# Strassen's seven products in the input projection of a conv and gMLP layer, with 1024-token blocks

## The chip, the cores and the metric

The kernel runs on one core of a Trainium2 chip. A time is that of one execution on the device in microseconds (us); the time shown for a kernel is the median of several. Engines: PE (TensorE, matrix products into PSUM), DVE (VectorE), ACT (ScalarE), POOL (GpSimd), and SP, whose queue issues nearly all DMAs. Each engine works through its own instructions in the order in which the program has them.

## The reference

```python
mod = c @ w_ada + b_ada
shift, scale, gate = jnp.split(mod, 3, axis=-1)
h = rmsnorm(x, g_pre) * (1.0 + scale) + shift          # 2048 tokens x 1024 channels
p = h @ w_in                                           # 8 projections of 1024 columns each
a = val * sigmoid(glu)                                 # val, glu, z, u, v, z2, gA, gB: columns of p
y = causal_depthwise_conv(a, conv_w) + conv_b          # 31 taps
y_a = (silu(layernorm(y)) * silu(z)) @ w_conv_out
v = layernorm(gelu(v))
s = einsum(tril(w_s), v) + b_s                         # per head, in chunks of 128 positions
y_b = (gelu(u) * s * silu(z2)) @ w_sgu_out
x = x + gate * ((sigmoid(gA) * y_a + sigmoid(gB) * y_b) @ w_o)
out = rmsnorm(x, g_final)
```

All is float32. PE gets the precision by parts: every operand is split into a high part (its copy in PE's 12-bit format, made by ACT) and a low part (what is left, a subtraction), and a product is three matmuls, high*high, high*low and low*high.

## The kernel before

The 2048 tokens go in four blocks of 512. In a block the kernel computes seven of the eight projections channel by channel (`unit`, L228: 128 columns against 512 tokens, 8 row tiles by 3 matmuls of 128x512, L232 to L234), and v token by token (`rows_unit`, L240, L244 to L246). The order in a block is: gate and value of the GLU, v, the other GLU pairs mixed with u and z2 (`step_uz`, which also does the position mixing, L588), then gB with w_b, z, gA with w_a, and w_o. That makes 56 + 16 units of the input projection and 24 units' worth of output products, 2112 matmuls of 128x512 a block and 8448 in all.

Weights come in pieces of 128x1024, loaded on SP's queue and split by ACT (L66) and DVE (L67), five pieces ahead at most (`take`, L213). The convolution is background work on DVE: 30 instructions of 128x512 for each of 8 channel tiles and each block (L487), read from a and accumulated in y, both in SBUF; two channel tiles take turns. They are spread between what DVE does for PE by `run_bg`, which lowers their priority. POOL does little: it copies 30 columns between blocks (L502, L505), and in the first 76 us it splits weights (L67) and scales x (L337).

In the first block the shift and scale of the conditioning come step by step: the products of c with w_ada are summed by DVE (L282, L286) and then over the partitions by PE (L296, L297), and each step's result feeds 21 matmuls of the first projections (L370, L371, L377). The LayerNorm sums over channels are pairs of matmuls with ones (`sums_of`, L107).

Of the kernel before, what the change touches and what calls it, by code (L numbers as in the profile page):

```python
# [7 lines left out]
F32 = mybir.dt.float32  # L8
# [4 lines left out]
PSUM = bass.MemoryType.PSUM  # L13

# [3 lines left out]
KT = D // P  # L18
T = 512
NB = SEQ // T  # L20
# [3 lines left out]
GC = 256  # L24
# [4 lines left out]
G_GLU, G_VAL = 0, 1  # L29
G_ZA, G_U, G_ZB, G_GA, G_GB = (8 + 4 * i for i in range(5))  # L30

# Columns of the packed per-channel parameters.
# [6 lines left out]
START = 7  # units whose sums the first block carries side by side, one bank each  # L39
LATER = 800  # by how much the background work yields to what is emitted after it  # L40
AHEAD = 5  # split weight pieces on chip
# [3 lines left out]
def hybrid_layer(  # L45
# [5 lines left out]
    ps = ctx.enter_context(tc.tile_pool(name="ps", bufs=8, space=PSUM))  # L51
# [3 lines left out]
    sm = ctx.enter_context(tc.tile_pool(name="sm", bufs=2))  # L55

    def bank():
        return ps.tile([P, 512], F32, tag="ps", name="bank")
# [3 lines left out]

    def split(dst, val, eng=nc.vector):
# [3 lines left out]
        eng.tensor_tensor(out=lo, in0=val, in1=hi.bitcast(F32), op=ALU.subtract)  # L67

# [9 lines left out]
    ones = const.tile([P, P], F32R, name="ones")  # L78
    nc.vector.tensor_copy(out=ones, in_=one.broadcast_to([P, P]))
# [3 lines left out]
    nc.gpsimd.memset(halo, 0.0)  # L83
    shift = const.tile([P, KT], F32, name="shift")
    gsc = const.tile([P, KT], F32, name="gsc")

    def rstd_of(ss, src):
        """ss <- 1 / sqrt(src / D + EPS)"""
        nc.scalar.activation(ss, src, AF.Sqrt, bias=eps_t, scale=1.0 / D)
        nc.vector.reciprocal(out=ss, in_=ss)  # L90

    def sums(val):
        """The sum of val over the partitions, on each of them: native float32."""
        pt = bank()
        nc.tensor.matmul(pt, ones.bitcast(F32), val, start=True, stop=True)  # L95
        return pt

    def parts(val):
        hi, lo = t512("hi", F32R), t512("lo", F32R)
        split((hi, lo), val)  # L100
        return hi, lo

    def sums_of(parts):
        """The same from the two parts; the ones are exact in one."""
        pt = bank()
        for i, part in enumerate(parts):
            nc.tensor.matmul(pt, ones, part, start=i == 0, stop=i == 1)  # L107
        return pt

# [1 line left out]
    def load_x(b):  # L111
        xn = big.tile([P, KT, T], F32, tag="yx", name="xn", bufs=1)
        for k in range(0, KT, 2):
            nc.sync.dma_start(
                out=xn[:, k : k + 2, :],
                in_=xt[k * P : (k + 2) * P, b * T : (b + 1) * T].rearrange(
                    "(k p) t -> p k t", p=P
                ),
            )
        return xn  # L120

    def squares_x(xn):
        rx = tmp.tile([P, T], F32, tag="rs", name="rx", bufs=1)
        for k in range(KT):
            if k == 0:
                nc.scalar.activation(rx, xn[:, k], AF.Square)
            else:
                q = t512("q")
                nc.scalar.activation(q, xn[:, k], AF.Square)
                nc.vector.tensor_tensor(out=rx, in0=rx, in1=q, op=ALU.add)  # L130
        return rx

    def make_ht(xn, rx, k):
        h = xn[:, k]
        nc.vector.tensor_tensor(out=h, in0=h, in1=rx, op=ALU.mult)
        nc.scalar.activation(
            h, h, AF.Identity, bias=shift[:, k : k + 1], scale=gsc[:, k : k + 1]
        )
        ht = big.tile([P, 2, T], F32R, tag="ht", name="ht", bufs=KT)
        split(ht, h)  # L140
        return ht

# [1 line left out]
    def pair(mat, g):  # L144
        return [mat[g, 0], mat[g, 1]]

    def rowsof(mat):
        return [mat[k * P : (k + 1) * P, :] for k in range(KT)]

    order = []  # L150
    for b in range(NB):
        if b == 0:
            order += [k for k in range(KT)]
            order += pair(w_in, G_VAL + 2)
        else:
            for g in range(4):
                order += pair(w_in, g)
        order += rowsof(w_v)
        for i, j in ((2, 0), (3, 1), (None, 2), (None, 3)):
            if i is not None:  # L160
                order += pair(w_in, G_GLU + 2 * i) + pair(w_in, G_VAL + 2 * i)
            order += pair(w_in, G_U + j) + pair(w_in, G_ZB + j)
        for i in range(4):
            order += pair(w_in, G_GB + i) + pair(w_b, i)
        for i in range(4):
            order += pair(w_in, G_ZA + i)
        for i in range(4):
            order += pair(w_in, G_GA + i) + pair(w_a, i)
        order += rowsof(w_o)
    ready = {}  # L170
    loaded = []
    state = {"prep": 0, "use": 0}

    def prep_load():
        n = state["prep"]
        state["prep"] += 1
        src = order[n]
        raw = wp.tile([P, 4 * GC], F32, tag="raw", name="raw", bufs=3)
        if isinstance(src, int):
            ks = slice(src % 4 * GC, (src % 4 + 1) * GC)  # L180
            half = src // 4
            nc.sync.dma_start(
                out=raw[:, : 3 * GC].rearrange("p (g c) -> p g c", c=GC),
                in_=w_in[0:3, half, :, ks].rearrange("g p c -> p g c"),
            )
            nc.sync.dma_start(
                out=raw[:, 3 * GC : START * P],
                in_=w_in[3, half, :, ks][:, : START * P - 3 * GC],
            )
        else:  # L190
            nc.sync.dma_start(out=raw, in_=src)
        loaded.append((n, raw))

    def prep_split():
        n, raw = loaded.pop(0)
        if n >= len(order) - (KT - AHEAD):
            # The last block's w_o stays whole; the input's tiles are free by then.
            ready[n] = []
            for h in range(2):
                w = big.tile([P, 2, T], F32R, tag="ht", name="wht", bufs=KT)  # L200
                split(w, raw[:, h * 512 : (h + 1) * 512])
                ready[n].append(w)
            return
        w = wp.tile([P, 2, 4 * GC], F32R, tag="whl", name="whl", bufs=AHEAD)
        ready[n] = w
        if n < KT:
            split(w[:, :, : START * P], raw[:, : START * P], nc.gpsimd)
        else:
            split(w, raw)

    def take(count):
        """The next pieces; whatever fits beside them is made too."""
        n = state["use"]  # L213
        state["use"] += count
        while loaded:
            prep_split()
        while state["prep"] < min(n + max(AHEAD, count), len(order)):
            prep_load()
            prep_split()
        return [ready.pop(n + i) for i in range(count)]  # L220

    def group():
        """The split weights of the next group: part, k tile -> [P, GC]."""
        hv = [w.rearrange("p s (k c) -> p s k c", c=GC) for w in take(2)]
        return lambda s, kt: hv[kt // 4][:, s, kt % 4, :]

    def unit(pt, w, sub, rhs):
        """pt[channel, token] = 128 columns of the group against rhs."""  # L228
        cs = slice(sub * P, (sub + 1) * P)
        for kt in range(KT):  # L230
            wh, wl = w(0, kt)[:, cs], w(1, kt)[:, cs]
            nc.tensor.matmul(pt, wh, rhs[kt][:, 0], start=kt == 0, stop=False)  # L232
            nc.tensor.matmul(pt, wh, rhs[kt][:, 1], start=False, stop=False)  # L233
            nc.tensor.matmul(pt, wl, rhs[kt][:, 0], start=False, stop=kt == KT - 1)  # L234

    def columns(w):
        """A piece of 1024 columns in halves."""
        return w if isinstance(w, list) else [w[:, :, n * 512 : (n + 1) * 512] for n in range(2)]
# [9 lines left out]
    def rows_units(pts, w, lhs, kt):  # L248
        w = columns(w)
        for (c, n), pt in pts.items():  # L250
            rows_unit(pt, w[n], lhs, kt, c)
# [570 lines left out]
```

## Time and profile before

| what | value |
|---|---|
| time, median of 3 runs | 2008.87 us (2008.4 to 2011.4) |
| span of the profiled execution, first to last instruction | 2006.4 us |
| PE busy | 98% |
| DVE busy | 79% |
| ACT busy | 41% |
| POOL busy | 6% |
| DMA, mean | 113 GB/s |

The profile is of one execution; the median of the runs is 2.5 us above its span, which is what lies around the first and the last instruction. A busy PE alone does not say that the kernel is bound by it: the rows of the windows and of the chain of waits have to show that no other engine's wait stands in between.

### The profile page before, as it was taken

The numbers are of one execution on the slowest core, as the hardware profiler recorded it, in microseconds if no ns is written. First come the engines' busy times: TensorE is split into PE (matmuls) and PEld (weight loads), VectorE is DVE, ScalarE is ACT, GpSimd is POOL, SyncE is SP. The second block draws the span as 40 slices with busy tenths as digits, with TensorE's granted clock in tenths as the row PEclk, the third lists the DMA queues.
The fourth block names the chain that finished last, engine by engine and source line by source line (L and its number), as shares of the span: only waits on it lengthen the run. The fifth ranks groups of instructions, "written<-read, shape, count | busy, mean of one in ns | idle before, by whom it ended". The sixth has DMA issues, their size and how long they took to land.

```text
span 2006.4 us, 22659 instructions
## 1 busy us (share of the span) xinstructions
PE 1970.9 (98%) x8784; PEld 1632.2 (81%) x8784; DVE 1581.3 (79%) x2158; ACT 813.0 (41%) x1021; POOL 129.5 (6%) x77
## 2 busy tenths in 40 slices
PE   5899999999999999999999999999999999999998
PEld 4688888888888888888888888888888888888886
DVE  7999999576499999367469999837638999964644
ACT  3433432465324343266332444236524343423632
POOL 3300000000001420000000012000000000000000
PEclk9999999999999999999999999999999999999999
DMA  7542222334242222224432222224343323232332
GB/s 277 196 139 95 84 95 95 105 135 138 99 143 95 84 95 95 97 72 162 143 137 95 95 95 93 86 94 136 106 139 134 100 90 98 91 98 92 103 112 79
DMA packets 67995, 226.55 MB, mean 113 GB/s; under 512 B 7088, under 2 KB 11312, under 8 KB 67888
## 3 DMA queue, kind: packets, MB, share of 16 engines
q1 hardware_dynamic: 67744, 224.95, 33.3%
q8 instruction: 68, 1.11, 0.2%
q14 instruction: 39, 0.32, 0.1%
q10 hardware_dynamic: 144, 0.16, 0.0%
HBM read 216.69 MB, written 8.39 MB: 112 GB/s over the span
## 4 chain that ended last, share of the span: by engine, by line
PE 95%; DMA 1%; DVE 1%; ACT 0%; issue 0%; ACTq 0%
PE bank L234 25%; PE bank L232 25%; PE bank L233 25%; PE bank L245 6%; PE bank L246 6%; PE bank L244 6%; PE bank L588 1%; DMA raw<-in_w_o 1%; PE bank L107 0%; DVE acc L286 0%; PE bank L95 0%; PE bank L377 0%; PE bank L371 0%; PE bank L370 0%; ACT wht L66 0%; DVE whl L67 0%
## 5 line engine op out<-in xcount | busy, mean ns | idle before, releaser
L232 PE MATMUL bank<-ht,whl 128*128 128x512 f32 x1736 | 678.7, 391 | 0.0
L234 PE MATMUL bank<-ht,whl 128*128 128x512 f32 x1736 | 675.5, 389 | 0.0
L233 PE MATMUL bank<-ht,whl 128*128 128x512 f32 x1736 | 675.5, 389 | 0.0
L487 DVE SCALAR_TENSOR_TENSOR y<-a,vec,y 128x512 f32<-128x512 f32 x960 | 658.1, 742 | 0.1
L67 DVE TENSOR_TENSOR whl<-raw,whl 128x1024 fp32r<-128x1024 f32 x343 | 418.3, 1221 | 268.3 <-ACT whl L66 267.9
L66 ACT ACTIVATE whl<-raw 128x1024 fp32r<-128x1024 f32 (+1 forms) x351 | 370.4, 1057 | 592.9 <-PE bank L234 326.2
L234 PEld LDWEIGHTS bank<-ht,whl 128*128 128x128 f32 x1736 | 325.9, 188 | 67.8
L233 PEld LDWEIGHTS bank<-ht,whl 128*128 128x128 f32 x1736 | 326.1, 188 | 66.8 <-issue 0.2
L232 PEld LDWEIGHTS bank<-ht,whl 128*128 128x128 f32 x1736 | 326.1, 188 | 66.7 <-issue 0.2
L502 POOL COPY a<-halo 128x30 f32<-128x30 f32 x32 | 61.8, 1951 | 900.1 <-DVE y L487 848.8
L246 PE MATMUL bank<-whl,ht 128*128 128x512 f32 x256 | 99.6, 389 | 0.0
L244 PE MATMUL bank<-whl,ht 128*128 128x512 f32 x256 | 99.6, 389 | 0.0
L232 PE MATMUL bank<-yb,whl 128*128 128x512 f32 x256 | 99.6, 389 | 0.0
L234 PE MATMUL bank<-yb,whl 128*128 128x512 f32 x256 | 99.6, 389 | 0.0
L233 PE MATMUL bank<-ya,whl 128*128 128x512 f32 x256 | 99.6, 389 | 0.0
L245 PE MATMUL bank<-whl,ht 128*128 128x512 f32 x256 | 99.6, 389 | 0.0
L233 PE MATMUL bank<-yb,whl 128*128 128x512 f32 x256 | 99.6, 389 | 0.0
L232 PE MATMUL bank<-ya,whl 128*128 128x512 f32 x256 | 99.6, 389 | 0.0
L234 PE MATMUL bank<-ya,whl 128*128 128x512 f32 x256 | 99.6, 389 | 0.0
L245 PE MATMUL bank<-whl,mg 128*128 128x512 f32 x232 | 90.3, 389 | 0.0
L244 PE MATMUL bank<-whl,mg 128*128 128x512 f32 x232 | 90.3, 389 | 0.0
L246 PE MATMUL bank<-whl,mg 128*128 128x512 f32 x232 | 90.2, 389 | 0.0
(144 smaller groups left out, 1928.6 us busy)
## 6 DMA issues: line engine op xcount, KB each, us to landing
raw<-in_w_in SPq DMA_DIRECT2D x218, 512.0 KB, 3.3
raw<-in_w_v SPq DMA_DIRECT2D x32, 512.0 KB, 3.4
raw<-in_w_b SPq DMA_DIRECT2D x32, 512.0 KB, 3.2
raw<-in_w_a SPq DMA_DIRECT2D x32, 512.0 KB, 3.5
raw<-in_w_o SPq DMA_DIRECT2D x32, 512.0 KB, 3.3
xn<-in_xt SPq DMA_DIRECT2D x16, 512.0 KB, 6.5
wa<-in_wada SPq DMA_DIRECT2D x16, 512.0 KB, 7.8
xo<-in_x SPq DMA_DIRECT2D x16, 512.0 KB, 5.6
```

What stands on the lines that cost most here:

```text
L66: nc.scalar.activation(hi, val, AF.Copy)
L67: eng.tensor_tensor(out=lo, in0=val, in1=hi.bitcast(F32), op=ALU.subtract)
L232: nc.tensor.matmul(pt, wh, rhs[kt][:, 0], start=kt == 0, stop=False)
L233: nc.tensor.matmul(pt, wh, rhs[kt][:, 1], start=False, stop=False)
L234: nc.tensor.matmul(pt, wl, rhs[kt][:, 0], start=False, stop=kt == KT - 1)
L244: nc.tensor.matmul(pt, xh, w[:, 0], start=kt == 0, stop=False)
L245: nc.tensor.matmul(pt, xh, w[:, 1], start=False, stop=False)
L246: nc.tensor.matmul(pt, xl, w[:, 0], start=False, stop=kt == KT - 1)
L487: nc.vector.scalar_tensor_tensor(out=yj, in0=a[:, k : k + T], scalar=col(V_CW, j * TAPS + k), in1=yj, op0=ALU.mult, op1=ALU.add,)
L502: nc.gpsimd.tensor_copy(out=a[:, :HALO], in_=halo[:, j, :])
L588: nc.tensor.matmul(pq[:, c * P : (c + 1) * P], vn[c][:, j * P : (j + 1) * P], wsT[:, j, :], start=True, stop=True,)
```

## The change

The whole function is written anew. What it does:

- **Blocks and the projection.** There are two blocks of 1024 tokens (s). Each of 28 `quad`s computes two column tiles (128 columns each) for both token halves by seven products of quarters instead of eight: each product is 4 row tiles by 3 matmuls, 84 matmuls in place of 96. Three operands of the products are sums of quarters of h (S1 to S4, made once a block on DVE), and the weights' sums (t1 to t4) are made for each quad from four raw pieces of 128x512. The results are added up in two PSUM banks; ACT copies three partial results a quad to SBUF (`snap`), DVE adds three times.
- **POOL** makes three of the four sums of weights and the low parts of six of the seven pieces of a quad; DVE makes those of t4.
- **Convolution.** 30 instructions of 128x1024 a channel tile, one chain at a time, accumulated in a PSUM tile of two banks (`cv`), with the first tap by ACT.
- **v first.** v is computed first, from two passes over each 512-token half; its split weights are written to memory in the first pass and read back whole (512 KB a piece of 12 matmuls), w_o likewise. The mixing results, the four gates' values and y_b go through memory and are loaded again.
- **adaLN.** Shift and scale are sums along rows on DVE (one instruction for 128x1024), with c on every partition; PE takes no part. The RMS and LayerNorm factors are made as columns: products with one (`col_sums`), root and reciprocal of 128x4, and `spread`, a diagonal matrix on DVE and a native float32 matmul.

```diff
+    def quad_piece(q, kind):
...
+            pool = nc.gpsimd
+            eng = nc.vector if kind == "t4" else pool
...
+            elif kind == "t1":
+                val = add(r(0, 0), r(0, 1), eng)
...
+            w = piece_tile()
+            split(w, val, eng)
...
+            a = bank()
+            prod(a, [take()], A11)
+            p1 = snap(a)
+            run_bg(2)
+            b = bank()
+            prod(b, [take()], A12)
+            tt(out=p1, in0=b, in1=p1, op=ALU.add)
+            c11(p1)
+            run_bg(2)
+            if pending:
+                pending.pop()()
+                run_bg(1)
+            c = bank()
+            prod(c, [take()], S1)
+            p5 = snap(c)
+            run_bg(2)
+            prod(a, [take()], S2, start=False)
+            p16 = snap(a)
...
+            prod(c, [take()], S4, start=False)
+            tt(out=p16, in0=c, in1=p16, op=ALU.subtract)
+            c12(p16)
...
+            prod(a, [take()], S3, start=False)
+            tt(out=p5, in0=p5, in1=a, op=ALU.subtract)
...
+            def end():
+                prod(a, [take()], A22, start=False)
+                c21(a)
...
+            def tap(k):
+                dst = a[:, :S] if k == HALO else cv[0]
+                nc.vector.scalar_tensor_tensor(
+                    out=dst, in0=a[:, k : k + S], scalar=col(V_CW, j * TAPS + k), in1=cv[0],
+                    op0=ALU.mult, op1=ALU.add,
+                )
...
+        v_half(pts, vn1, st1, 1)
+        mv1 = v_aggr(st1)
+        came = v_norm(vn1, mv1)[:, 0:1]
+        mixing(1, vn1, wsT, sbias)
...
+        for j in range(KT):
+            glu(j)
+            uz(j)
+            spilled(AF.Sigmoid, d_sa[j], d_sbg[j])
+        for i in range(KH):
+            spilled(AF.Silu, d_sz[2 * i], d_sz[2 * i + 1])
...
+        def ln_rstd(h):
+            hh = slice(h * T, (h + 1) * T)
+            pc = bank()
+            col_sums(rsq[0][:, hh], pc, 0, NC)
+            pr = spread(rstd_cols(pc[:, :NC], NC))
```

Three places of the programs' order, where a row is a line of the kernel, an operation, and the tile that it writes and those that it reads. The first is DVE in the middle of the projections. Before, two channel tiles of the convolution take turns (a is the input with its halo, y the sum, vec the taps' weights):

```order
L487 SCALAR_TENSOR_TENSOR y_3841<-a_4119,vec_73,y_3841 128x512 [waits DVE_49]
L67 TENSOR_TENSOR whl_4361<-raw_4359,whl_4361 128x1024 [waits DMAHW1_49,Activation_49]
L487 SCALAR_TENSOR_TENSOR y_3841<-a_4083,vec_73,y_3841 128x512 [waits DVE_49]
L487 SCALAR_TENSOR_TENSOR y_3841<-a_4119,vec_73,y_3841 128x512 [waits DVE_49]
L487 SCALAR_TENSOR_TENSOR y_3841<-a_4083,vec_73,y_3841 128x512 [waits DVE_49]
```

Now one chain in cv stands between the sums of the quads (L634, L648, L652), the gates (L732, L733) and t4's pieces (L88, L223):

```order
L676 SCALAR_TENSOR_TENSOR a_1741<-a_1741,vec_75,cv_1945 128x1024 [waits DVE_49]
L687 TENSOR_TENSOR s1_2327<-a_1310,a_1741 128x1024 [waits DVE_49]
L715 TENSOR_TENSOR a_2202<-snap_2284,sg_2403 128x512 [waits Activation_49]
L676 SCALAR_TENSOR_TENSOR cv_2408<-a_2202,vec_75,cv_2408 128x1024 [waits DVE_49,Activation_49]
L88 TENSOR_TENSOR whl_2454<-raw_2267,whl_2454 128x512 [waits PE_49,Activation_49]
L676 SCALAR_TENSOR_TENSOR cv_2408<-a_2202,vec_75,cv_2408 128x1024 [waits DVE_49]
L648 TENSOR_TENSOR snap_2449<-bank_2410,snap_2449 128x512 [waits PE_49]
L676 SCALAR_TENSOR_TENSOR cv_2408<-a_2202,vec_75,cv_2408 128x1024 [waits DVE_49] x2
L732 TENSOR_TENSOR snap_2367<-snap_2367,snap_2449 128x512 [waits Activation_49]
L652 TENSOR_TENSOR snap_2428<-snap_2428,bank_2348 128x512 [waits DMAHW1_49,PE_49]
```

The convolution of one channel tile ends just ahead of the row (L715) that gives the input of the next, so it fills the three quads between two GLU quads. The second place is POOL. Before it has, in the middle of the kernel, only copies of the halo:

```order
L502 COPY a_4575<-halo_81 128x30 [waits DVE_49,Activation_49,Pool_49]
L502 COPY a_4611<-halo_81 128x30 [waits DVE_49,Activation_49,Pool_49]
L505 COPY halo_81<-a_4575 128x30 [waits DVE_49,Pool_49]
L505 COPY halo_81<-a_4611 128x30 [waits DVE_49,Pool_49]
L502 COPY a_4916<-halo_81 128x30 [waits DVE_49,Activation_49]
```

Now it has nine instructions of 128x512 for a quad, here those of one quad (raw are its four raw pieces, whl split pieces):

```order
L88 TENSOR_TENSOR whl_1808<-raw_1806,whl_1808 128x512 [waits DVE_49,DMAHW5_49,PE_49,Activation_49]
L223 TENSOR_TENSOR raw_1806<-raw_1806,raw_1866 128x512 [waits DMAHW0_49,Pool_49]
L223 TENSOR_TENSOR raw_1866<-raw_1866,raw_1886 128x512 [waits DMAHW5_49,Pool_49]
L88 TENSOR_TENSOR whl_1829<-raw_1827,whl_1829 128x512 [waits DMAHW6_49,PE_49,Activation_49]
L88 TENSOR_TENSOR whl_1869<-raw_1806,whl_1869 128x512 [waits Activation_49]
L223 TENSOR_TENSOR raw_1806<-raw_1806,raw_1886 128x512 [waits Pool_49]
L88 TENSOR_TENSOR whl_1889<-raw_1806,whl_1889 128x512 [waits Activation_49]
L88 TENSOR_TENSOR whl_1907<-raw_1886,whl_1907 128x512 [waits PE_49,Activation_49]
L88 TENSOR_TENSOR whl_1925<-raw_1866,whl_1925 128x512 [waits Activation_49]
```

The halo copies have left POOL. The third place is PE behind v. Before, the next GLU products follow v's last matmuls, and the mixing comes four units later:

```order
L244 MATMUL bank_4137<-whl_4253,ht_3795 128x512
L245 MATMUL bank_4137<-whl_4253,ht_3795 128x512
L246 MATMUL bank_4137<-whl_4253,ht_3795 128x512
L232 MATMUL bank_4472<-ht_3557,whl_4289 128x512 [waits Activation_49]
L233 MATMUL bank_4472<-ht_3557,whl_4289 128x512
```

Now the mixing (L432) of the second token half stands right behind its v products (L312 to L314), and the quads come after it:

```order
L312 MATMUL bank_1023<-whl_1066,h_791 128x512
L313 MATMUL bank_1023<-whl_1066,h_791 128x512
L314 MATMUL bank_1023<-whl_1066,h_791 128x512
L432 MATMUL bank_1198<-wsT_730,vn_807 128x128 [waits DVE_49,PE_49]
L432 MATMUL bank_1206<-wsT_730,vn_807 128x128 [waits PE_49]
L432 MATMUL bank_1198<-wsT_730,vn_808 128x128 [waits DVE_49]
```

Nothing is left on PE between v's last product and the first instruction that reads v's normalized values. In the same way each `col_sums` (L146) of the convolution's LayerNorm is followed directly by its `spread` (L161).

## Rows read from the trace of the kernel before

**Rows 1.** The page: busy time, share of the span and instructions of each engine.

```profile
PE 1970.9 (98%) x8784; PEld 1632.2 (81%) x8784; DVE 1581.3 (79%) x2158; ACT 813.0 (41%) x1021; POOL 129.5 (6%) x77
```

**Rows 2.** Windows: busy us (instructions) of PE, PEld, DVE, ACT, POOL; clock, DMA.

```profile
0.00:100.00 100.00, 71.98 (x290) 57.08 (x291) 86.75 (x128) 35.48 (x44) 33.23 (x29) 0.95 0.68 236
20.00:24.00 4.00, 3.61 (x10) 2.91 (x11) 3.63 (x5) 1.18 (x2) 2.74 (x2) 1.00 1.06 386
661.93:1149.35 487.42, 487.42 (x2185) 404.81 (x2184) 381.13 (x513) 202.24 (x252) 47.59 (x16) 1.00 0.32 108
1999.00:2006.40 7.40, 0.01 (x1) 0.00 (x0) 2.63 (x5) 1.74 (x4) 0.00 (x0) 0.77 0.19 71
```

**Rows 3.** The chain that ended last, in order: start us, us, engine, tile, line.

```profile
76.88 0.61 PE bank L297 x4
...
154.74 3.43 PE bank L95 x8
...
174.52 0.89 PE bank L588 x8
...
449.30 0.46 PE bank L107 x2
...
661.93 0.89 PE bank L588 x8
```

**Rows 4.** Timeline of DVE: start us, us, engine, line, operation, shapes, count.

```profile
227.66 0.67 DVE L67 TENSOR_TENSOR yb<-r,yb 128x512 fp32r<-128x512 f32 x1
228.27 0.67 DVE L515 TENSOR_TENSOR s<-s,y 128x512 f32<-128x512 f32 x1
228.87 0.67 DVE L585 TENSOR_TENSOR z<-z,gu 128x512 f32<-128x512 f32 x1
229.47 0.73 DVE L593 SCALAR_TENSOR_TENSOR r<-bank,vec,sbias 128x512 f32<-128x512 f32 x1
...
547.75 4.87 DVE L753 SCALAR_TENSOR_TENSOR xo<-xo,ss,gfin 128x1024 f32<-128x1024 f32 x4
```

**Rows 5.** Instructions of lines 286, 282, 502, 337: ns min/median/max, first and last start.

```profile
L286 DVE SCALAR_TENSOR_TENSOR acc<-wa,vec,acc x52: 469/477/2270, 12.9 to 76.3; 128x256 f32<-128x256 f32 x52
...
L282 DVE TENSOR_SCALAR acc<-wa,vec x8: 346/2194/2211, 12.5 to 64.4; 128x256 f32<-128x256 f32 x8
...
L502 POOL COPY a<-halo x32: 202/1047/13297, 1.2 to 1655.4; 128x30 f32<-128x30 f32 x32
...
L337 POOL TENSOR_TENSOR xn<-xn,rx x7: 1311/1335/1482, 23.3 to 74.5; 128x512 f32<-128x512 f32 x7
```

**Rows 6.** Groups by line and shape: busy us, mean ns of one, idle before.

```profile
L286 DVE SCALAR_TENSOR_TENSOR acc<-wa,vec,acc 128x256 f32<-128x256 f32 x52 | 32.9, 677 | 0.4
L282 DVE TENSOR_SCALAR acc<-wa,vec 128x256 f32<-128x256 f32 x8 | 12.1, 1508 | 0.2 <-DMA wa<-in_wada 0.2
L67 POOL TENSOR_TENSOR whl<-raw,whl 128x896 fp32r<-128x896 f32 x8 | 17.2, 2156 | 47.6 <-ACT whl L66 33.3 <-issue 14.4
```

**Rows 7.** The same, of the steps of v's normalization.

```profile
L555 DVE BATCH_NORM_STATS2 st<-vn 128x6 f32<-128x512 f32 x32 | 19.9, 662 | 0.0
L554 ACT ACTIVATE vn<-bank 128x512 f32<-128x512 f32 x32 | 16.1, 629 | 0.0
L561 DVE TENSOR_SCALAR vn<-vn,mv,rs 128x1024 f32<-128x1024 f32 x16 | 11.9, 804 | 0.0
L558 ACT ACT_TABLE_LOAD x4 | 5.1, 1283 | 0.1
```

**Rows 8.** Timeline of PE behind a pause in the start: start us, us, form.

```profile
21.41 0.63 PE L370 MATMUL bank<-ht,whl 128*128 128x512 f32 x1
21.84 0.63 PE L371 MATMUL bank<-ht,whl 128*128 128x512 f32 x1
...
24.14 0.40 PE L370 MATMUL bank<-ht,whl 128*128 128x512 f32 x1
24.38 0.39 PE L371 MATMUL bank<-ht,whl 128*128 128x512 f32 x1
```

More of the change, by code (lines that the diff above doesn't have):

```diff
@@ new lines, in col_sums, with spread @@
+    def col_sums(val, pt, first, n):
+        for c in range(n):
+            nc.tensor.matmul(
+                pt[:, first + c : first + c + 1], val[:, c * P : (c + 1) * P], one,
+                start=True, stop=True,
+            )
+    def spread(cols):
+        diag = t512("diag")
+        nc.vector.tensor_tensor(
+            out=diag.rearrange("p (c t) -> p c t", t=P),
+            in0=ident.rearrange("p (c t) -> p c t", c=1).broadcast_to([P, NC, P]),
+            in1=cols.rearrange("p (c t) -> p c t", t=1).broadcast_to([P, NC, P]),
+            op=ALU.mult,
+        )
+        pt = bank()
+        nc.tensor.matmul(pt, ones, diag, start=True, stop=True)
+        return pt
@@ L92, in sums @@
     def sums(val):
         pt = bank()
-        nc.tensor.matmul(pt, ones.bitcast(F32), val, start=True, stop=True)
+        nc.tensor.matmul(pt, ones, val, start=True, stop=True)
         return pt
[L98 to L108, printed above, removed]
@@ L133, in make_ht @@
[L133 to L148, printed above, removed]
+                out=cache[k][n], in_=w.bitcast(F32).rearrange("p s c -> p (s c)")
+            )
@@ L150, in hybrid_layer @@
+    NQ = 28
     order = []
[L151 to L154, printed above, removed]
-        else:
[L156 to L169, printed above, removed]
@@ L211, in take @@
[L211 to L234, printed above, removed]
@@ L321, in hybrid_layer, with v_pass @@
+    def v_pass(lhs, n_banks=NC):
+        pts = [bank() for _ in range(NC)]
+        for kt in range(KT):
+            w = take()
+            for c in range(NC):
+                rows_unit(pts[c], w, lhs, kt, c)
+        return pts
+    xn = [xtile("xn") for _ in range(KT)]
+    cbc = hs32("cbc")
+    nc.sync.dma_start(out=cbc, in_=rows[:, 3 * D : 4 * D].broadcast_to([P, D]))
+    A = [[], []]
+    wa = {0: load_ada(0)}
+    load_xn(0, 0, xn)
     with tc.manual_schedule(engines=MANUAL):
@@ new lines, in hybrid_layer, with scaled @@
+        prep_to(2)
+        wa[1] = load_ada(1)
+        prx = spread(rstd_cols(pc[:, :NC], NC))
+        rx = t512("rx")
+        nc.scalar.activation(rx, prx, AF.Copy)
+        def scaled(k):
+            v = xn[k][:, :T]
+            nc.vector.tensor_tensor(out=v, in0=v, in1=rx if k else prx, op=ALU.mult)
+            t = hs("h")
+            modulated(t[:, 0], v, k)
+            modulated(v, v, k)
+            A[0].append(t)
+        scaled(0)
+        cvt = wide()
+        first = [bank() for _ in range(6)] + [cvt[:, :T], cvt[:, T:]]
@@ new lines, in hybrid_layer, with next_rstd @@
+        if last:
+            out_half(0)
+            finish_last(1, *out_last(1))
+            break
+        xn = [xtile("xn") for _ in range(KT)]
+        for k in range(KT):
+            after(xn[k][:, 0:1], rsq[0][:, 0:1])
+        for h in range(2):
+            load_xn(s + 1, h, xn)
+        A = [[], []]
+        rxs = []
+        def next_rstd(ss, xn=xn):
+            r = t512("rx")
+            after(r[:, 0:1], came)
+            nc.scalar.activation(r, spread(token_rstd(ss)), AF.Copy)
+            rxs.append(r)
```

1164 lines of the change are left out of this document (667 added, 497 removed).

## Prediction

> **What bounds the kernel now.** The page comes first [rows 1]: PE is busy for 98% of the span, DVE for 79%. A busy PE proves little, so I looked at one block in the windows [rows 2]: PE is busy for all of 487.42 us, at a clock of 1.00. The reader is to see there that no gap is left in the middle. The chain in order [rows 3] confirms it: the block's first mixing group comes at 174.52 and again at 661.93, 487.41 later, as far apart as in the windows. A block is 2112 matmuls, 8 mixing groups of 0.89 and 3 pairs of sums of 0.46, so a matmul costs (487.41 - 7.12 - 1.38) / 2112 = 0.2268 us. PE's stream is the bound, and work taken from it counts in full as long as nothing else comes to the front.
>
> What is lost lies at the two ends. Ahead of the first mixing group stand 552 matmuls (125.2 us) and sums of 3.43 us; 174.5 - 125.2 - 3.4 = 45.9 us went to the start. Behind the last matmul the tail takes 7.4 us [rows 2].
>
> **The gain.** 56 quads save 12 matmuls each: 672 x 0.2268 = 152.4 us. Against it stand more native float32 sums. One of them costs 3.43 / 4 = 0.86 us and a group of four one-column products twice 0.61 us [rows 3]. The change has 15 of the first (12.9 us) and 5 of the second (6.1 us), before had 8.5 us of sums behind the start: 10.5 us more. With both ends as they are, the span would be 2006.4 - 152.4 + 10.5 = 1864.5 us. Everything from here on is what PE loses on top of that.
>
> **DVE between the quads.** This is the term that decides. Three quads last 252 x 0.2268 = 57.2 us on PE. By the order, DVE has 31 instructions of 1024 columns for them (30 taps and one sum) and 23 of 512. Four 1024-column instructions of that kind start (4.87 - 1.28) / 3 = 1.20 us apart; short ones start 0.60 apart [rows 4]. A tap that directly follows the tap whose result it needs starts only when that is done, 1.28 and a gap of 0.04, so 0.12 later, and in the order 15 of 31 do: 31 x 1.20 + 15 x 0.12 = 39.0 us, and 23 x 0.60 + 3 x 0.12 = 14.2 us. That is 53.2 us of 57.2.
>
> The next price is a wait that the old kernel had only in its start. POOL gets 27 instructions in the three quads, 1.34 us each [rows 5], or 36 us of about 59. DVE and POOL shut each other out: a copy of 30 columns on POOL takes 0.2 us at best and 13.3 at worst between taps that read SBUF twice, and DVE's sums of the conditioning take 0.47 us as a rule and up to 2.27 while POOL runs [rows 5]. By the means [rows 6], 52 of them lost 0.20 us each and 8 lost 1.16, so 19.7 us over 60, or 0.33 each, with POOL busy for a third of the time [rows 2] in pieces of 2.16 us. For pieces of 1.34 us at 61% that scales to 0.33 x 1.85 x 0.62 = 0.38 us. 15 of DVE's instructions read SBUF twice; the taps read SBUF once and PSUM once. 15 x 0.38 = 5.7 us.
>
> That the taps stay out of this is a choice, since no row shows a tap with its sum in PSUM beside a busy POOL. The Trainium skill (SBUF — State Buffer, Who interferes with whom) says that a DVE instruction with at most one SBUF input does not meet GpSimd at the shared port; the trace agrees as far as instructions with two inputs are the ones that show the loss. By that rule the taps pay nothing, and the sum goes by nothing.
>
> Of what PSUM costs a tap, rows show only reading: the instruction with one operand in PSUM (L593) starts 0.60 behind its forerunner and takes 0.73 like other short ones of its kind [rows 4]; the writing has no row. I take zero; one more gap of 0.12 a tap (3.6 us) is the other end. The Trainium skill (Perfetto Trace Analysis, Optimizing Scalar/DVE Operations) gives DVE about 125 ns of overhead an instruction on PSUM against 60 on SBUF; by it, as an estimate, 2 us would come to each three quads and 28 us to the whole. No run here shows it yet.
>
> So DVE needs about 58.9 us where PE needs 57.2, and waits of its own for PE and ACT, in an order fixed beforehand, keep it from being full: I count 2.1 us a round. Seven rounds a block carry a convolution behind them (the eighth has the four z quads as slack): 14 x 2.1 = 30 us. The ends: without any wait at the port and without the 0.12 gaps it is 51 us and PE hides it (0 us); if each of the 15 waits for a whole POOL instruction it is 73 us and costs 14 x 16 = 224 us. I stay near the scaled mean, which comes from the same pair of engines.
>
> **Waits on PE that are new.**
> - Behind v. In the order the mixing follows v's last product. Between them lie four Gelus (4 x 0.63), statistics 0.66, a table load 1.28 and a root 0.3, and a scaling 0.80, with the other three scalings partly in the way [rows 7]: 7 to 11 us, I take 9, twice: 18 us. Before, four units of the GLU stood there and hid it.
> - LayerNorm. A spread waits for its columns: sum, root, reciprocal, diagonal, some 3 us each, and the first also for a DVE that has 22 instructions to do since the mean: 5 + 3 us, twice: 16 us (10 to 30).
> - Behind such pauses PE starts slowly: in the start, matmuls begin 0.43 us apart at first, its lower level of 1.2 GHz, and 0.24 apart from 24.1 us on [rows 8], though the window's granted clock reads 1.00. Seven at 0.43 lose 1.5 us; six pauses: 9 us.
>
> **Transfers and ends.** The most that the DMAs moved is 386 GB/s, 20 to 24 us into the run [rows 2]. The start has to bring the weights of shift and scale, pieces of v and their copies back to memory, x twice: about 24.5 MB up to the last of the eight steps, 64 us; with 10 us of work behind it the first pass ends near 78 us, having done 192 matmuls (43.5 us). The second token half's input then holds PE up for some 8 us: 43 us lost in place of 45.9. I write 0 (-8 to +15). The output of the first block moves about 19.5 MB in a half that lasts 43.5 us on PE: 51 us, +7 (0 to 20). Loading y_b between quads and products: +4. DVE in the first block's v passes: +4. At the end six pieces of w_o come late: +4 (0 to 10).
>
> **The sum.** 1864.5 + 30 + 18 + 16 + 9 + 0 + 7 + 4 + 4 + 4 = 1956.5 us of span, and with 2.5 us around it, as before, 1959 us.
>
> **The rivals.**
> - DVE keeps up. POOL's instructions are then spread so that few meet, and the ends of the pauses are short: 1959 - 30, and up to 30 less if the other terms lie at their lower ends: 1895 to 1929 us. For it: DVE at 53 of 57 us. Against it: the 13.3 us of [rows 5].
> - DVE takes over as the bound: slower than before from the point where a round takes 57.2 + (2008.9 - 1929) / 14 = 62.9 us, since nothing else then matters. 31 taps with a gap each and half a POOL instruction for each double reader come to 53.2 + 3.6 + 10 = 67 us, which gives 1929 + 14 x 9.6 = 2063 us.
> - The taps do shut POOL out, as the old ones did. Then each of POOL's 27 instructions stands in DVE's line: 53 + 36 = 89 us a round, 1929 + 14 x 32 = 2380 us. [Rows 5] has POOL waiting that long, but for taps with two operands in SBUF.
> - The products get fewer, but PE is held up a little everywhere, a quad waiting for a snap or a piece, and the pace falls by 10% in the 56 quads: 1067 us becomes 1170, and the sum 2060 less the 30 of DVE: 2030 us. Against it: each piece is asked for four products (11 us) ahead.
>
> **How the numbers follow.** My forecast, 1930 to 1995 us, has 0.54; DVE keeping up 0.20; DVE as the bound 0.15, of which 0.03 still below the old time and 0.03 level with it; POOL shut out 0.05; the slow pace 0.06, half of it level or faster. The range from 1890 to 2040 us leaves out POOL shut out, the worse half of DVE as the bound, and a little below. Faster by over 0.2%, about what a measurement of this kernel can tell from no change, is 0.54 + 0.20 + 0.03 + 0.02 = 0.79; level 0.04; slower 0.17.
>
> **What would show it.** Right: 7776 matmuls of 128x512, a quad of 19 to 20 us with taps 1.2 to 1.3 us apart, double readers on DVE of up to 2 us beside POOL, and in PE's chain one pause of about 9 us behind v in each block. Wrong: a DVE that is not above 90% between the quads, POOL's instructions far above 1.4 us, taps above 1.35, or PE waiting for SP's queue in the output stage for more than 20 us.

## The result

The changed kernel takes 2030.09 us (median of 4 runs, 2025.4 to 2031.8) against 2008.97 us before in the same runs: a ratio of 1.0101, 95% interval 1.0087 to 1.0115. It is slower by 1%. The time lies inside the range from 1890 to 2040 us, but on the other side of the old time: the forecast of 1959 us and of "faster" was wrong.

First the page of the changed kernel, its busy times; it answers to [rows 1]:

```profile
PE 1862.5 (92%) x8102; PEld 1513.3 (75%) x8102; DVE 1464.7 (72%) x1791; ACT 902.0 (44%) x1418; POOL 704.3 (35%) x511
```

PE has 682 instructions fewer, 672 of them the saved matmuls, but it is busy for 92% of a span of 2027.1 us and no longer for 98%. So the work did leave PE, and PE now stands idle for part of the time. The windows say where. I cut them where PE passes from one stage to the next (columns as in [rows 2]):

```profile
0.00:92.60 92.60, 56.91 (x202) 40.85 (x202) 48.41 (x95) 35.38 (x61) 1.88 (x7) 0.94 0.94 326
92.60:133.70 41.10, 26.55 (x101) 20.61 (x101) 29.81 (x58) 21.18 (x31) 0.00 (x0) 0.79 0.72 208
133.70:176.50 42.80, 37.77 (x225) 33.65 (x224) 23.25 (x47) 13.24 (x24) 10.25 (x8) 0.96 0.43 149
176.50:746.90 570.40, 548.80 (x2360) 446.94 (x2359) 489.85 (x479) 301.94 (x463) 340.27 (x244) 0.98 0.31 106
746.90:937.00 190.10, 183.62 (x794) 148.89 (x792) 123.02 (x201) 67.64 (x105) 0.00 (x0) 0.98 0.70 230
937.00:1070.10 133.10, 92.65 (x391) 73.86 (x390) 65.17 (x115) 50.46 (x90) 0.00 (x0) 0.85 0.72 251
1070.10:1135.40 65.30, 65.30 (x290) 54.07 (x289) 18.29 (x30) 15.33 (x24) 0.00 (x0) 1.00 0.67 228
1179.10:1742.40 563.30, 542.60 (x2358) 439.62 (x2358) 497.45 (x471) 302.07 (x463) 341.62 (x244) 1.00 0.31 107
1931.20:2027.10 95.90, 87.72 (x385) 71.72 (x383) 37.08 (x86) 16.25 (x35) 0.00 (x0) 0.99 0.67 253
```

Each stage has a known number of matmuls at 0.2268 us; what its window lasts beyond them is the loss. The 288 matmuls of v in block 1 show that the scale is right: 65.3 us of work in 65.30 us. By it the losses are:

| place | window | work on PE | lost | predicted |
|---|---|---|---|---|
| start, to the first mixing group at 133.7 | 133.7 | 65.3 + 1.7 (sums) | 66.7 | 45.9 |
| behind v, block 0 and 1 | 42.8, 43.7 | 21.8 + 14.3 each | 14.3 | 18 + part of the restarts |
| 28 quads, block 0 and 1 (0.9 us of y_b's products among them) | 570.4, 563.3 | 533.4 + 0.9 each | 65.1 | 30 |
| w_b and w_a, block 0 and 1 | 190.1, 188.8 | 173.2 each | 32.5 | 20, and the native sums |
| output stage, block 0 | 133.1 | 87.1 | 46.0 | 7 |
| output stage, block 1, with the end | 95.9 | 87.1 | 8.8 | 11.4 |

Three rows are far off: the quads by 35 us, the output stage of block 0 by 39 and the start by 21. Together that is 95 us, of which the smaller terms give 24 back; the remaining 71 us are what the span of 2027.1 lies above the 1956.5 of the sum.

What PE waited for names the same places (who waited, for whom; us in total, times, longest):

```profile
PE bank L297 <- ACT snap L625: 40.1, 35, 2.9
PE bank L161 <- DVE rx L92: 25.2, 1, 25.2
PE bank L161 <- DVE diag L154: 22.7, 6, 13.8
PE bank L146 <- DVE acc L478: 16.1, 1, 16.1
PE bank L312 <- ACT vn L571: 14.5, 1, 14.5
PE bank L432 <- DVE vn L405: 10.1, 2, 5.0
```

**The quads.** One convolution has to fit beside three quads; I call these three quads a round. One round of block 1 lasts 61.28 us, the next 61.33. In that time DVE is busy for 97% (window from the end of one convolution to the next):

```profile
1511.74:1573.02 61.28, 58.34 (x253) 46.90 (x254) 59.39 (x55) 32.83 (x51) 38.00 (x28) 1.00 0.28 95
```

PE's longest wait for a snap in this round, 1.66 us, is for ACT, but ACT had waited 2.48 us for DVE just before, to split what DVE's L733 makes (first two rows ACT, then PE):

```profile
1535.13 0.63 ACT L87 ACTIVATE hi<-g 128x512 fp32r<-128x512 f32 x1 [2.48 <-DVE g L733]
1535.67 1.07 ACT L625 ACTIVATE snap<-bank 128x512 f32<-128x512 f32 x2
1536.30 0.51 PE L297 MATMUL bank<-s,whl 128*128 128x512 f32 x1 [1.66 <-ACT snap L625]
```

DVE's own groups in two rounds show what fills it:

```profile
L676 DVE SCALAR_TENSOR_TENSOR cv<-a,vec,cv 128x1024 f32<-128x1024 f32 x58 | 74.4, 1283 | 3.5 <-ACT cv L670 2.6
L88 DVE TENSOR_TENSOR whl<-raw,whl 128x512 fp32r<-128x512 f32 x6 | 10.0, 1662 | 0.0
L223 DVE TENSOR_TENSOR raw<-raw 128x512 f32<-128x512 f32 x6 | 8.1, 1342 | 0.2
L715 DVE TENSOR_TENSOR a<-snap,sg 128x512 f32<-128x512 f32 x3 | 5.3, 1782 | 0.0
L648 DVE TENSOR_TENSOR snap<-bank,snap 128x512 f32<-128x512 f32 x6 | 4.1, 680 | 0.0
L732 DVE TENSOR_TENSOR g<-g,snap 128x512 f32<-128x512 f32 x2 | 2.5, 1257 | 0.0
```

L648 has one operand in PSUM and takes 0.68 us. The other groups shown below the taps have both in SBUF: the low part of t4 takes 1.66, its sum 1.34, the gate L715 1.78. Their excess over 0.68, with that of the smaller groups, is 7.1 us a round where the prediction took 5.7. The first tap waits 1.3 us for ACT. Without these two DVE needs 61.3 - 7.1 - 1.3 = 52.9 us; the prediction had worked out 53.2.

**The output stage.** PE's timeline behind its 96th matmul with w_o:

```profile
958.96 0.39 PE L314 MATMUL bank<-whl,mg 128*128 128x512 f32 x1
984.52 2.07 PE L161 MATMUL bank<-diag,ones 128*128 128x512 f32 x2 [25.17 <-DVE rx L92]
1000.42 2.07 PE L161 MATMUL bank<-diag,ones 128*128 128x512 f32 x2 [13.84 <-DVE diag L154]
1001.51 1.41 PE L312 MATMUL bank<-whl,mg 128*128 128x512 f32 x1
```

The two L161 are the spreads of the row factors of the next block's tokens. They stand in PE's order among the products with w_o, wait for sums of squares whose tokens are still being loaded, and everything behind them waits along. The loads of these tokens (xs, 16 in all) stand on SP's queue behind the writes of w_o's split pieces (d_wo); the first is issued at 964.95, when PE has already stopped:

```profile
944.68 12.11 SPq L185 DMA_DIRECT2D d_wo<-whl  x6
963.26 1.00 SPq L185 DMA_DIRECT2D d_wo<-whl  x2
964.95 2.21 SPq L78 DMA_DIRECT2D xs<-in_x  x3
980.01 7.91 SPq L78 DMA_DIRECT2D xs<-in_x  x7
```

**The start.** The chain of waits at its end, in order (start us, us, what):

```profile
87.56 0.08 DVE s L346
87.67 0.31 ACT cols L139
88.00 0.19 DVE cols L140
88.20 10.41 DMA d_rx<-cols
98.68 5.01 DMA rx<-d_rx
103.72 0.70 DVE xn L356
```

The row factors of the second 512 tokens go through memory and take 15.4 us on the way, with PE idle behind them.

### The profile page after: what moved, and what is told of

Its sections match the earlier page's. It is cut to its first block, busy times and chain, and to the rows that moved or that the text cites. A ratio compares the mean times of both kernels' runs of the same rounds, so it can differ in the third digit from the quotient of the medians.

```text
span 2027.1 us, 23381 instructions
## 1 busy us (share of the span) xinstructions
PE 1862.5 (92%) x8102; PEld 1513.3 (75%) x8102; DVE 1464.7 (72%) x1791; ACT 902.0 (44%) x1418; POOL 704.3 (35%) x511
## 4 chain that ended last, share of the span: by engine, by line
PE 49%; DVE 27%; DMA 9%; issue 7%; ACT 4%; POOL 2%; SPq 1%; ACTq 0%; DVEq 0%; POOLq 0%
DVE cv L676 14%; PE bank L297 11%; PE bank L303 11%; PE bank L300 11%; PE bank L312 4%; PE bank L313 4%; PE bank L314 4%; POOL whl L88 2%; DVE whl L88 2%; PE bank L432 2%; ACT whl L87 1%; DVE raw L223 1%; DVE snap L634 1%; DVE a L715 1%; DMA xs<-in_x 1%
## 5 line engine op out<-in xcount | busy, mean ns | idle before, releaser
L88 POOL TENSOR_TENSOR whl<-raw,whl 128x512 fp32r<-128x512 f32 x336 | 463.1, 1382 | 927.2 <-ACT whl L87 893.1
L676 DVE SCALAR_TENSOR_TENSOR cv<-a,vec,cv 128x1024 f32<-128x1024 f32 x464 | 595.2, 1283 | 34.1 <-ACT cv L670 26.8
L87 ACT ACTIVATE whl<-raw 128x512 fp32r<-128x512 f32 x488 | 302.0, 626 | 354.2 <-PE bank L303 205.3
L297 PE MATMUL bank<-s,whl 128*128 128x512 f32 x896 | 356.9, 398 | 40.1 <-ACT snap L625 40.1
L300 PE MATMUL bank<-s,whl 128*128 128x512 f32 x896 | 352.3, 393 | 0.0
L303 PE MATMUL bank<-s,whl 128*128 128x512 f32 x896 | 351.9, 393 | 0.0
L303 PE MATMUL bank<-h,whl 128*128 128x512 f32 x672 | 262.9, 391 | 2.2 <-POOL whl L88 2.2
L297 PE MATMUL bank<-h,whl 128*128 128x512 f32 x672 | 262.0, 390 | 0.0
L300 PE MATMUL bank<-h,whl 128*128 128x512 f32 x672 | 261.6, 389 | 0.0
L223 POOL TENSOR_TENSOR raw<-raw 128x512 f32<-128x512 f32 x168 | 242.4, 1443 | 11.3
L297 PEld LDWEIGHTS bank<-s,whl 128*128 128x128 f32 x896 | 170.2, 190 | 90.1 <-ACT snap L625 55.5
L88 DVE TENSOR_TENSOR whl<-raw,whl 128x512 fp32r<-128x512 f32 x152 | 144.8, 958 | 84.3 <-ACT whl L87 81.5
L303 PEld LDWEIGHTS bank<-s,whl 128*128 128x128 f32 x896 | 170.4, 190 | 36.4
L300 PEld LDWEIGHTS bank<-s,whl 128*128 128x128 f32 x896 | 170.5, 190 | 34.5
L303 PEld LDWEIGHTS bank<-h,whl 128*128 128x128 f32 x672 | 126.1, 188 | 32.6 <-POOL whl L88 6.5
L297 PEld LDWEIGHTS bank<-h,whl 128*128 128x128 f32 x672 | 126.2, 188 | 27.1 <-issue 0.9
L300 PEld LDWEIGHTS bank<-h,whl 128*128 128x128 f32 x672 | 126.2, 188 | 26.0
L625 ACT ACTIVATE snap<-bank 128x512 f32<-128x512 f32 x168 | 97.4, 589 | 84.4 <-PE bank L303 84.4
L223 DVE TENSOR_TENSOR raw<-raw 128x512 f32<-128x512 f32 x56 | 63.6, 1136 | 59.4 <-POOL whl L88 58.3
```

What stands on the lines that cost most here:

```text
L223: eng.tensor_tensor(out=dst, in0=dst, in1=src, op=ALU.add)
L297: nc.tensor.matmul(pt, wh, h[:, 0], start=start and k == 0, stop=False, skip_group_check=True)
L300: nc.tensor.matmul(pt, wh, h[:, 1], start=False, stop=False, skip_group_check=True)
L303: nc.tensor.matmul(pt, wl, h[:, 0], start=False, stop=k == last, skip_group_check=True)
L625: nc.scalar.activation(t, pt, AF.Copy)
L676: nc.vector.scalar_tensor_tensor(out=dst, in0=a[:, k : k + S], scalar=col(V_CW, j * TAPS + k), in1=cv[0], op0=ALU.mult, op1=ALU.add,)
```

## The experiments

Medians are of 4 or 5 runs where an interval is given; the changed kernel (2030.1 us) is what they are compared with, unless another is named. The numbers in brackets are the ratio to the kernel before and its 95% interval.

**t4 on POOL.**

```diff
-            eng = nc.vector if kind == "t4" else pool
+            eng = pool
```

> t4's sum and low part go to POOL, which then makes all of them; 6 instructions a round leave DVE, all of which read SBUF twice. Theory B (DVE is the bound between the quads, full at 61.3 us a round): DVE loses six times 1.3 to 1.7 us, so it needs 52 to 54 us a round, PE's 57.2 is then the longest, a round takes 57.3 to 58.5 us, and the time falls by 14 x 3 to 4 = 40 to 55 us, to 1975 to 1990 us. POOL goes from 36 to 44 us a round. Rival C (the engines' fixed orders hold PE up through snaps and pieces, DVE is full only because it is waited for): the round stays within 1 us of 61.3 and the time within 15 us of 2030. Rival D (the port moves the loss: with a third more of its work POOL is held up by DVE and delivers late): round over 62, time above 2040 us.

Measured: 1979.73 us (0.985, 0.9835 to 0.9865), 50 us less. A round now goes from one L715 to the next in 57.96 us. PE is busy for 57.42 of them and DVE for 51.21, and DVE waits 3.84 us for ACT's sigmoid, a reader of PE's products:

```profile
1469.35 0.69 DVE L715 TENSOR_TENSOR a<-snap,sg 128x512 f32<-128x512 f32 x1 [3.84 <-ACT sg L699]
1469.35:1527.31 57.96, 57.42 (x254) 47.24 (x253) 51.21 (x48) 33.22 (x51) 46.36 (x33) 1.00 0.30 100
```

PE's waits for snaps go from 40.1 to 9.6 us. Nearly all of the gain lies in the quads of the two blocks (26.7 and 22.5 us). Theory B holds: DVE was the bound between the quads, and most of these waits were its.

**Fewer instructions on POOL.**

```diff
             def add(dst, src, eng):
+                if eng is nc.gpsimd:
+                    return dst
                 eng.tensor_tensor(out=dst, in0=dst, in1=src, op=ALU.add)
```

> POOL's three sums a quad are left out (t1 to t3 are then a raw piece each, so the projections come out other than the reference's); DVE's work is as in the changed kernel. POOL has 18 instructions a round and not 27. Theory B, port part (of DVE's 61.3 us a round 7.1 are waits of instructions that read SBUF twice while POOL runs): two thirds of that remain, so a round takes 58.5 to 59.5 us and the time is 1990 to 2003 us. Rival (DVE's long instructions are long for another reason, such as what they follow): the round stays at 61.3 and the time at 2020 to 2035 us.

Measured: 1981.8 us (one run), a round of 58.12 us. DVE's own instructions are the same ones, but the low parts of t4 are back at 0.68 us and its sum at 1.04; the excess of all that read SBUF twice is 3.5 us and not 7.1:

```profile
L225 DVE TENSOR_TENSOR raw<-raw 128x512 f32<-128x512 f32 x3 | 3.1, 1042 | 0.5 <-POOL whl L88 0.5
L88 DVE TENSOR_TENSOR whl<-raw,whl 128x512 fp32r<-128x512 f32 x3 | 2.0, 682 | 0.0
L717 DVE TENSOR_TENSOR a<-snap,sg 128x512 f32<-128x512 f32 x1 | 1.8, 1781 | 0.0
```

So the length of DVE's instructions does come from POOL's beside them. Their excess fell by half where theory B took a third, and the time lies below its 1990 to 2003 us. Which instructions meet may matter more than how many there are; no run separates the two.

**Taps that read SBUF twice.**

```diff
-scalar=col(V_CW, j * TAPS + k), in1=cv[0],
+scalar=col(V_CW, j * TAPS + k), in1=a[:, :S],
```

> Every tap takes its second operand from a (in SBUF) and no longer from cv; it still writes cv in PSUM. The convolution's sum is left out with that: each tap adds a to its product. Theory P (a DVE instruction with two operands in SBUF and POOL shut each other out, one with an operand in PSUM does not): POOL's 27 instructions of a round stand in DVE's line or wait for its end, a round takes 53 + 36 = 89 us in place of 61.3, and the time is 2300 to 2450 us, POOL's instructions with maxima far above 1.8 us. Rival (the operands' place is nothing, POOL's and DVE's losses come from the sharing of SBUF as a whole): POOL stays at 1.4 us, taps at 1.28 us, and the time within 30 us of 2030.

Measured: 2317.91 us (one run), a round of 80 us. First the taps and POOL's low parts of the changed kernel (ns min/median/max), then those of this one:

```profile
L676 DVE SCALAR_TENSOR_TENSOR cv<-a,vec,cv x464: 1248/1282/1293, 206.3 to 1690.0; 128x1024 f32<-128x1024 f32 x155
L88 POOL TENSOR_TENSOR whl<-raw,whl x336: 1263/1296/1823, 152.7 to 1726.0; 128x512 fp32r<-128x512 f32 x168
```

```profile
L676 DVE SCALAR_TENSOR_TENSOR cv<-a,vec x464: 1253/1719/2376, 207.8 to 1974.0; 128x1024 f32<-128x1024 f32 x155
L88 POOL TENSOR_TENSOR whl<-raw,whl x336: 1262/1736/2388, 154.1 to 2014.3; 128x512 fp32r<-128x512 f32 x168
```

Theory P holds, with the loss shared: a tap becomes 0.44 us longer at the median and so does POOL's instruction; neither is shut out for many in a row, and a round is 80 us, not 89. By this one run the accumulator in PSUM is worth nearly 290 us here.

**The next block's statistics later.** The edit takes the two spreads and the scaling out of the list for the first token half and puts them into that for the second:

```diff
         out_half(0)
+        bg.extend(norms)
         out_half(1)
```

> In the first block's output stage the two spreads of the next block's row factors, and the scaling of its tokens, come behind the first token half's products of w_o instead of among them. Theory A: PE stands 25 and 14 us there because its order has these spreads in front of products whose operands are there, and the statistics are late on SP's queue. Then the stage from the first product with w_o to the first of the next v lasts 133.1 - 39 = 94 us (87.1 of products) up to 100, and the time is 1991 to 1998 us. Rival: the stage is bound by its transfers (33.4 MB; at 330 GB/s, as they ran up to 970 us, 101 us): then it ends at 105 to 112 us and PE waits for pieces of w_o instead; time 2003 to 2010 us. If DVE or ACT cannot finish the scaled tokens in the second half, PE waits ahead of v in block 1 for up to 20 us.

Measured: 2022.42 us (1.007, 1.0047 to 1.0094), the stage still 128 us. Neither forecast came: PE's two waits moved along, 17.4 and 18.2 us, now in the second half.

```profile
1017.02 2.08 PE L161 MATMUL bank<-diag,ones 128*128 128x512 f32 x2 [17.38 <-DVE rx L92]
1037.27 2.07 PE L161 MATMUL bank<-diag,ones 128*128 128x512 f32 x2 [18.17 <-DVE diag L154]
```

In this kernel's order the loads of the tokens had moved too, behind all but three pieces of w_o on SP's queue. So the edit could not tell the theories apart. It showed what the next one had to hold fixed.

**The next block's statistics earlier.** The loads and squares stand beside the products with w_a; the spreads stay:

```diff
             bg.extend(lambda r=r, n=n: gate_step(r, n) for r in range(KT) for n in range(2))
+            nss = []
+            for h in range(2):
+                ss, sq = token_stats(s + 1, h)
+                nss.append(ss)
+                bg.extend(sq)
```

> The loads and squares of the next block's tokens run beside the products with w_a, before the first copy of w_o is written; the spreads stay where they were. The earlier run that only moved the spreads took the loads along to the end of SP's queue, and PE waited 17 and 18 us there. Theory A, mended: the statistics are late because their loads stand on SP's queue behind the writes of w_o, which wait for splits. Then PE's waits of 25 and 14 us fall to 3 to 6 us in all, the stage lasts 95 to 102 us in place of 133.1, and the time is 1993 to 2002 us. Rival (the transfers bound the stage): PE then waits for pieces of w_o or for the next block's tokens, the stage stays above 110 us, time above 2007 us.

Measured: 1993.11 us (0.9923, 0.9908 to 0.9938), 37 us less. The stage is 91.4 us long, and PE waits for nothing in it but 1.8 us for a piece of w_o:

```profile
943.60:1035.00 91.40, 89.63 (x391) 73.01 (x390) 63.52 (x112) 35.85 (x55) 0.00 (x0) 1.00 0.91 328
```

The loads are now issued from 882.6 to 913.3 us, ahead of the writes. The DMAs run at 328 GB/s and hold up little, so the rival falls as well: the 39 us of waits were the place of 16 loads in a queue. The stage is 42 us shorter and the kernel 37; the other 5 were lost elsewhere.

**v's pieces written in the second pass.**

```diff
-            order += [make_row(w_v, d_wv, k, n) for k in range(KT) for n in range(2)]
-            order += [load_row(d_wv, k, n) for n in range(2) for k in range(KT)]
+            order += [make_row(w_v, d_wv, k, n, False) for k in range(KT) for n in range(2)]
+            order += [make_row(w_v, d_wv, k, n) for n in range(2) for k in range(KT)]
```

> The split weights of v are written to memory in the second pass of the first block (which splits raw pieces again) and not in the first, so 8 MB of writes leave the start. Theory E: in the start each step's weights of the conditioning stand on SP's queue behind writes that wait for DVE's splits, and behind 8 MB of traffic; the first mixing group, at 133.7 us, comes 15 to 25 us earlier, and the time is 2005 to 2015 us. Rival: the start is bound by the chain of each step (sum along the row, scaling, subtraction, products) or by the round trip of the second half's row factors through memory (10.4 + 5.0 us); then the first mixing group comes less than 6 us earlier and the time stays at 2024 to 2030 us. The second pass could lose up to 5 us to its own splits.

Measured: 2017.98 us (1.0042, 1.0028 to 1.0056), 12 us less, between the two. The first pass ends 10 us sooner (82 us against 92) and so does the first quad's start (166.2 against 176.5); the first mixing group, now at 114 us, overtakes part of v's products in this order and can't be compared. So the writes cost 10 us and not up to 25; that the chain of each step keeps the rest is not shown.

**The second mixing behind two products.**

```diff
-        pending = []
+        pending = [mix_and_sums]
```

> The mixing of the second token half, and the sums S2 to S4 behind it, come after the first two products of the first quad instead of right behind v. Theory F: PE's 6.7 and 7.6 us behind v are the norm chain alone, and two products (24 matmuls, 5.4 us) cover most of it: 2 x 5 us less and about 2 us less at the lower clock, time 2017 to 2022 us. Rival: the S2 to S4 splits, now made later, hold up the fourth product of that quad by as much; time 2026 to 2034 us.

Measured: 2018.34 us (1.0046, 1.0031 to 1.0061), 12 us less, in the range of theory F. What is lost from the second pass to the third product goes from 14.3 to 6.5 us over the two blocks; the other 4 us are not placed.

**The LayerNorm's spread apart from its columns.** The spread becomes a step of its own, four steps of background work later:

```diff
-            pr = spread(rstd_cols(pc[:, :NC], NC))
-            nc.scalar.activation(rsq[0][:, hh], pr, AF.Copy)
+            lnc[h] = rstd_cols(pc[:, :NC], NC)
+
+        def ln_spread(h):
+            hh = slice(h * T, (h + 1) * T)
+            nc.scalar.activation(rsq[0][:, hh], spread(lnc[h]), AF.Copy)
```

> The spread of the convolution's LayerNorm factors comes four steps of background work behind its columns and not directly behind. Theory G: PE's waits there (some 2 us each for the diagonal, 2 to 3 us for the sum of squares, in the profile 17 and 16 us lost in the two stages with native sums counted in) fall by 2 us a spread, 6 to 9 us in all with the restarts: time 2021 to 2025 us. Rival: the wait only moves to the products with w_a, whose operands come later: 2027 to 2034 us.

Measured: 2036.92 us (1.0142, 1.0123 to 1.0161), 7 us more. Theory G failed, and the time lies above the rival's too. The columns slid down PE's order with the spread, six of the eight at 777.40 and the spread's wait behind them:

```profile
777.40 0.72 PE L146 MATMUL bank<-one,rsq 128*128 128x1 f32 x6
780.80 2.03 PE L161 MATMUL bank<-diag,ones 128*128 128x512 f32 x2 [2.67 <-DVE diag L154]
```

Its longest wait grew from 1.9 to 2.8 us. All the waits there come to 3 us more in block 0 and 2 more in block 1; the rest of the 7 is not placed.

**Together.** All five edits, and all but the last:

> t4 on POOL, v's pieces written in the second pass, the second mixing behind two products, the next block's statistics beside w_a and the spreads of the LayerNorm apart, all together. If the four places are independent, the gains add: 50 + 12 + 12 as measured, 30 to 35 and 6 to 9 as expected, 110 to 118 us below 2030: 1912 to 1920 us, below the kernel before by 4.5%. Rival: they share a resource (the DMAs around the output stage, ACT between the quads), and a third of the gain is lost: 1945 to 1955 us.

> The same as the run of all together, without the split of the LayerNorm's spread, which alone was 7 us slower. If that loss is the same beside the others, 1925.6 - 5 to 8 = 1918 to 1921 us. Rival: the 7 us were the spread of the start and of the transfers from build to build (first mixing between 133.7 and 137.8 us in the runs so far); then 1923 to 1929 us.

Measured: 1925.59 us (0.9579, 0.9563 to 0.9595) and 1922.9 us (0.9563, 0.9547 to 0.9579). The single gains of the four, 50 + 12 + 12 + 37, make 111 us, and 107 came: the places are nearly independent. Both times lie above their forecasts, which had counted on the split or on its loss. The two kernels differ by less than their runs scatter, so the 7 us of the split alone stay open.

**The row factors through PE.** Besides the four edits, the second token half's factors of the start come by a spread into the first bank that is read:

```diff
-                with nc.allow_non_contiguous_dma(reason="a column per chunk"):
...
-                rx1 = t512("rx1")
-                nc.sync.dma_start(out=rx1, in_=d_rx.broadcast_to([P, T]))
...
+                        nc.scalar.activation(rx1, spread(rs1), AF.Copy)
```

> The run without the split, and the second token half's row factors come through PE (a diagonal and a spread in the first bank that is read) and not through memory (10.4 and 5.0 us in the profile). Theory H: the 14.5 us for which PE waits ahead of the second half are this round trip; the chain Gelu, spread, copy, scaling and h is some 6 us, so 6 to 9 us are saved: 1910 to 1914 us. Rival: the wait is for ACT's Gelus and table load, which stand in the same place, and nothing is saved (within 2 us).

Measured: 1907.94 us (0.9491, 0.9476 to 0.9505), 15 us below the kernel without it. The first quad starts 9.6 us sooner (139.5 against 149.2), a little over what theory H gave; the other 5 us lie in stages that the edit doesn't touch, most of them beside w_b and w_a, and stay unexplained. This version is 5.1% faster than the kernel before.

## Why the prediction was wrong

Three terms of the sum were too small: DVE between the quads by 35 us, the output of the first block by 39, the start by 21. In the first the mechanism was right and its size was off; in the second the mechanism itself was missing.

- **The gain** came as worked out: 7776 matmuls at the old pace, and 65.30 us where 65.3 were due.
- **DVE between the quads** was the right mechanism with the wrong size. Its needs without the port (53.2 against 52.9 us) and the taps (1.20 us apart behind other instructions, 1.32 behind their own) were right. "15 x 0.38 = 5.7 us" should have been 7.1 us, and the wait for ACT's first tap, 1.3 us, had no term of its own. So a round is 61.3 us, 4.1 above PE's 57.2 and not 2.1; 14 of them are 57 us. The other 8 of the 65.1 go with block 0, whose quads lose 7 us more than block 1's and where the clock fell (below). Of the rivals, "DVE takes over as the bound" is what the chip does, and moving six instructions away shows it; but at 61.3 us it stays below the 62.9 that this rival needed to make the kernel slower by itself.
- **The output stage** is the step that failed in its mechanism. "The output of the first block moves about 19.5 MB ... +7" priced its bytes and not its order. The list of new waits on PE has the mixing behind v and the spreads of the convolution's LayerNorm, but not the two spreads of the next block's factors, which stand among the products with w_o. PE waited 39 us there, and the run that moves their loads takes 37 back. A sign that the prediction names, PE waiting there for SP's queue for more than 20 us, was seen in this form without having been priced.
- **The start**, "I write 0", cost 21 us: the first pass ended at 92.6 us and not near 78, with 30 MB moved at 326 GB/s and not 24.5 MB at 386, and for the second token half's input, whose row factors took 15.4 us through memory, PE waited 14.5 us where the sum had some 8. The two edits there brought the first quad 10 us forward each.
- **The taps in PSUM** paid nothing for POOL and nothing for PSUM. For the first, the rule of the Trainium skill that I cited (SBUF — State Buffer, Who interferes with whom) is borne out from both sides: 1.25 to 1.29 us for all 464 taps, and 1.72 at the median once their second operand is in SBUF. The prediction's remark that in the old trace it was the instructions with two inputs that showed the loss is not right: L282 there reads one tensor and was among them, with 2.19 us at the median and 0.35 at best [rows 5]. For the second, the other rule of the Trainium skill (Perfetto Trace Analysis, Optimizing Scalar/DVE Operations) would, as an estimate, have put 2 us on each round; the taps start 1.20 us apart, as 1024 columns in SBUF did in [rows 4], and no run here shows that overhead.
- **The terms that came out smaller**: behind v 14.3 us with its restarts, DVE in the first v passes 0, the end 2.6 less.

Either of the two larger terms turned the sign by itself: without the waits in the output stage the kernel takes 1993.1 us, with t4 on POOL 1979.7, and both are faster than before.

That the time lies inside the range, and close to the 2030 us of the rival with the slow pace, is luck. That rival had the 56 quads slower by 10%, some 103 us; they lost 65.1, and the rest was lost in the output stage and at the start, which it doesn't name.

## What to carry over

When work on PE shrinks, list every instruction that remains in its order and waits for another engine, those of the next block too, and follow each operand back to its load on the queue: 39 us here were 16 loads standing behind writes. DVE looked 93% full in a sum of durations and was full here, once its instructions that read SBUF twice met a busy POOL (7.1 us a round) and one wait for ACT came on top; giving six of them to POOL took most of the loss away, and one operand in PSUM kept the taps out of it. An edit that moves a step can move its loads too, so look at the order of the queue before believing what the edit tests.

## What was not expected of the hardware

POOL and DVE share the loss nearly evenly when both read SBUF twice: 0.44 us each at the median, 2.38 and 2.39 at most, where the kernel before had shown a POOL copy of 13.3 us between its taps [rows 5].

Around four short pauses PE's clock came down between stretches in which it was busy throughout. Windows around four of PE's waits for a snap (2.9 us each) in the quads of block 0 show a granted clock below 1:

```profile
466.00:478.00 12.00, 9.15 (x28) 6.76 (x27) 10.60 (x10) 3.57 (x8) 6.47 (x4) 0.72 0.35 125
530.00:540.00 10.00, 7.13 (x23) 5.11 (x22) 9.77 (x9) 2.71 (x6) 6.50 (x4) 0.83 0.41 135
593.00:603.00 10.00, 7.12 (x24) 5.21 (x23) 9.55 (x9) 2.72 (x5) 5.83 (x4) 0.83 0.33 115
655.00:666.00 11.00, 8.13 (x23) 5.86 (x23) 9.61 (x9) 2.65 (x5) 5.96 (x4) 0.69 0.28 98
```

That is its lower level, 1.2 GHz, for some 56, 34, 34 and 62% of each. In the kernel before the same stretches read 1.00 with PE busy throughout. In the quads of block 1, where PE's longest wait for a snap is 1.7 us, the whole window reads 1.00.
